# Masks in a row on GpSimd, a bank's last copy on ScalarE, fused gate terms, and attention parts emitted later, in a one-core streaming encoder step

## The chip, the cores and the metric

The kernel runs on one core of a Trainium2 chip. The metric is the device time of one execution in microseconds (us); the median of three runs is given with the lowest and highest. One execution was also recorded by the hardware profiler. Engines are named as in the profile: PE (TensorE matmul), PEld (its weight load), DVE (VectorE), ACT (ScalarE), POOL (GpSimd) and SP (SyncE, which issues the transfers).

## What is computed

One layer of an encoder runs on two request groups, 512 prompt rows and 64 sample rows (576 columns in the kernel), with shared weights in float32. The part that the change touches is the first third:

```python
xn = _rmsnorm(x, p['ln_mix'])
proj = xn @ p['w_in']
conv_in, z, a, b, qd, kd, vd = jnp.split(proj, SPLIT_AT, axis=-1)
c, conv_new = _causal_conv(conv_in, p['conv_w'], conv_buf)
c = jax.nn.silu(c.astype(jnp.float32))
...
g = -jnp.exp(p['a_log']) * jax.nn.softplus(a + p['dt_bias'])
beta = jax.nn.sigmoid(b)
oa, S_new = _gdn_chunked(qa, ka, va, g, beta, S0)
oa = _rmsnorm(oa, p['gdn_norm']) * jax.nn.silu(z)
```

`_gdn_chunked` is a gated delta rule over chunks of 64 rows: per chunk it forms products of keys, scales them with `exp` of differences of cumulated gates, and solves a lower triangular system. Behind it come a differential attention, the output projection, an attention over a memory of 256 rows (whose keys and values are projected here too), and a feed-forward block of width 4096.

## The kernel before

All activations stay on the chip, transposed: 128 features by 576 columns. Every weight matrix is read in tiles of 128x1024 and split into a high part (`wh`, a cast on ACT, L161) and a low part (`wl`, a subtraction on DVE, L162); a projection of 128 output columns is then three products, high by high, high by low and low by high. `project` (L170) does it in two halves, of 256 columns and of 320, each into a bank of the tag `pr`; there are three such banks. `evac` then takes a half out of its bank: the first half with a copy on ACT (L194) and an addition on DVE (L195), the second with two operations, on its first 256 and its last 64 columns.

The time line of the first third: the convolution's inputs are projected in blocks of 128 channels (`conv_input`, L314 to L323), each followed by the four convolution terms (ACT L455, DVE L457) and a silu (ACT L459, L460). Then the gates are computed from two small projections: softplus as an exponential (L525) and a series on DVE (L526 to L538), which ends in `gg` (L548), then cumulated sums on PE and exponentials for `beta`, `egl` and `kdc` (ACT L549, L569, L571, L590). Then four z blocks are projected (`project_z`, with the silu in L647 for a half's 256 columns and L649 for the last 64), with the memory's rows normed beside them (the squares in L223, transposes into `u` in L900). Beside the z blocks, `gdn_prep` prepares chunks two by two (c = 0 and 1 first): squares of keys and queries (ACT L682, L686), the exponential `gam` (ACT L701), the split of the system `At` (ACT L757), products on PE, and a solve that doubles block sizes from 1 to 64, for which a constant matrix `lev` of 128x128 holds at which level a pair of rows is joined (used in L734 and L764).

`lev` is built from masks of blocks of 2, 4, ... 128 rows. In the kernel before, POOL makes one mask (a fill and two affine selects, L605 to L608), DVE subtracts the one before (L610) and adds the difference to `lev` (L614), seven times.

The program's order is not the order in which the code emits it. A scheduler places the emitted instructions on the engines by dependence and its own costs; the code steers it with `tc.issue_after(i)` (what is emitted inside comes behind instruction i), `tc.high_priority()` and `tc.keep_in_program_order`. Each engine runs its own queue in order. On ACT, the functions come in table sets, and an ACT_TABLE_LOAD stands in the queue wherever the next function needs another set: silu and the exponential need different ones here, copies and squares need none.

Of the kernel before, what the change touches and what calls it, by code (L numbers as in the profile page):

```python
# [11 lines left out]
ALU = mybir.AluOpType  # L12
# [3 lines left out]
P = 128  # L16
# [3 lines left out]
DEC = 64  # L20
# [6 lines left out]
SOFF = 515  # L27
# [10 lines left out]
def hybrid_layer_kernel(  # L38
# [10 lines left out]
    V, A, G = nc.vector, nc.scalar, nc.gpsimd  # L49
# [29 lines left out]
    def nm(s):  # L79
        uid[0] += 1  # L80
        return f"{s}_{uid[0]}"

    def pair(slot, dt=F32):

        return up.tile([P, 2, 4, T], dt, tag=f"u{slot}", name=nm("u"))

    def view(u, i, a, b):
        return u[:, i].rearrange("p k t -> p (k t)")[:, : a * b].rearrange("p (a b) -> p a b", a=a)
# [3 lines left out]
    def small(tag, shape, bufs=None, dt=F32):  # L92
        tag = SHARED.get(tag, tag)
        bufs = 1 if tag in ("vn", "on", "S") or tag[:-1] in ("At", "Dt", "Y") else 2
        return sp.tile(shape, dt, tag=tag, name=nm(tag), bufs=bufs)
# [4 lines left out]
    def bank(tag="ba"):  # L100
        return ps.tile([P, 512], F32, tag=tag, name=nm(tag), bufs=BANKS[tag])

    def const(shape, name, dt=F32):
        return cp.tile(shape, dt, tag=name, name=name)
# [32 lines left out]
    ident = const([P, P], "ident")  # L137
# [17 lines left out]
    def split_weights(w, shape):  # L155
        raw = wp.tile(shape, F32, tag="raw", name=nm("raw"), bufs=3)
        nc.sync.dma_start(raw, w.rearrange("(k p) n -> p k n", p=P))
        wh = wp.tile(shape, F32R, tag="wh", name=nm("wh"))
        wl = wp.tile(shape, F32R, tag="wl", name=nm("wl"))
        with tc.high_priority():  # L160
            A.copy(wh, raw)  # L161
            V.tensor_tensor(wl, raw, wh.bitcast(F32), ALU.subtract)  # L162
        return wh, wl
# [29 lines left out]
    def add_to(dst, b, more):  # L193
        A.copy(dst, more)  # L194
        V.tensor_tensor(dst, b, dst, ALU.add)  # L195
# [116 lines left out]
    def conv_input(m, tag="cb"):  # L312
        cbs[m] = cb = small(tag, [P, 584])
        G.memset(cb[:, 0:3], 0.0)  # L314

        def evac(b, a0, n, more):
            if a0 == 0 and more is None:
                A.copy(cb[:, 3:259], b)
            elif a0 == 0:
                add_to(cb[:, 3:259], b, more)  # L320
            else:
                A.copy(cb[:, 3 + a0 : 259 + a0], b[:, :256])
                V.tensor_copy(cb[:, SOFF + 3 : SOFF + 3 + DEC], b[:, 256:])  # L323

        return evac

# [113 lines left out]
    for typ in (1, 0, 2):  # L440
# [3 lines left out]
        for h in range(H):  # L444
            m = typ * 4 + h
# [5 lines left out]
            cb = cbs[m]  # L451
# [6 lines left out]
            last_v = nc.cur_bb.bb.instructions[-1]  # L458
# [6 lines left out]
        if typ == 1:  # L465
            behind_keys = last_v, last_g
# [27 lines left out]
    for a0, n in HALVES:  # L494
        b = bank("pr")
# [7 lines left out]
    b = bank()  # L503
# [13 lines left out]
    def gt(tag):  # L517
        return const([P, 5, 4], tag)

    pre, gg, beta = gt("pre"), gt("gg"), gt("beta")  # L520
    t1, t2, t3 = gt("t1"), gt("t2"), gt("t3")
# [5 lines left out]
    V.reciprocal(t2, t2)  # L527
    V.tensor_tensor(t1, t1, t2, ALU.mult)
    V.tensor_tensor(t2, t1, t1, ALU.mult)
    V.tensor_scalar(t3, t2, 1.0 / 17, 1.0 / 15, ALU.mult, ALU.add)  # L530
    for d in (13, 11, 9, 7, 5, 3, 1):
        V.tensor_tensor(t3, t3, t2, ALU.mult)
        V.tensor_scalar(t3, t3, 1.0 / d, None, ALU.add)
    V.tensor_tensor(t3, t3, t1, ALU.mult)
    V.tensor_scalar(pre, pre, 0.0, None, ALU.max)
    V.scalar_tensor_tensor(t3, t3, 2.0, pre, ALU.mult, ALU.add)
    V.tensor_tensor(t3, t3, ea.unsqueeze(1).to_broadcast([P, 5, 4]), ALU.mult)
# [16 lines left out]
    for j in range(3):  # L554
        b = bank()
# [40 lines left out]
    mn = view(e5, 0, 2, D)  # L596
    mhl = pair(4, F32R)
    mh, ml = view(mhl, 0, KT, NMEM), view(mhl, 1, KT, NMEM)
    with tc.issue_after(behind_keys[0]), tc.issue_after(behind_keys[1]):
        lev = const([P, P], "lev")  # L600
        prev = ident
        for lb in range(7):
            s = 2 << lb
            e = small("X", [P, P])
            G.memset(e, 1.0)  # L605
            ev = e.rearrange("p (n s) -> p n s", s=s)
            G.affine_select(out=ev, in_=ev, pattern=[[-s, P // s], [0, s]], compare_op=ALU.is_ge, fill=0.0, base=0, channel_multiplier=1)  # L607
            G.affine_select(out=ev, in_=ev, pattern=[[s, P // s], [0, s]], compare_op=ALU.is_ge, fill=0.0, base=s - 1, channel_multiplier=-1)  # L608
            m = small("B0", [P, P])
            V.tensor_tensor(m, e, prev, ALU.subtract)  # L610
            if lb == 0:
                V.tensor_copy(lev, m)
            else:
                V.scalar_tensor_tensor(lev, m, float(1 << lb), lev, ALU.mult, ALU.add)  # L614
            prev = e

# [461 lines left out]
    for w, out in ((w_mem_k, o_mk), (w_mem_v, o_mv)):  # L1080
        dst = tokens
        for f in range(2):
            fs = slice(512 * f, 512 * f + 512)
            bs = [bank("pr") for _ in range(2)]
            for kc in range(4):
                wt = split_weights(w[0, 256 * kc : 256 * kc + 256, fs], [P, 2, 512])
                for k in (2 * kc, 2 * kc + 1):
                    for t in range(2):
                        ts_ = slice(t * P, (t + 1) * P)
                        for j, (wi, x) in enumerate(((0, mh), (0, ml), (1, mh))):  # L1090
                            mm(
                                bs[t], x[:, k, ts_], wt[wi][:, k % 2, :],
                                start=(k == 0 and j == 0), stop=(k == KT - 1 and j == 2),
                            )
            for t in range(2):
                (A.copy if t else V.tensor_copy)(dst[:, t, fs], bs[t])
                if out is o_mv:
                    A.copy(mv[:, t, fs], dst[:, t, fs])
                    V.tensor_tensor(mvl[2 * t + f], dst[:, t, fs], mv[:, t, fs].bitcast(F32), ALU.subtract)
            if out is o_mk:  # L1100
                for i in range(2):
                    b = bank()
                    for j in range(2):
                        m = 4 * f + 2 * i + j
                        for t in range(2):
                            tr(b[:, j * 256 + t * P : j * 256 + (t + 1) * P], dst[:, t, m * P : (m + 1) * P])
                    m = 4 * f + 2 * i
                    split_turned(mkT[:, m : m + 2, :], mkl[m // 2].rearrange("p (j n) -> p j n", j=2), b)
            nc.sync.dma_start(out[0, 0].rearrange("(b p) h d -> p b (h d)", p=P)[:, :, fs], dst[:, :, fs])
            if out is o_mk and f == 1:  # L1110
                finish()

                ob = pair(5, F32R)
                for h in range(H):
                    split_to((ob,), od[:, h, :], h, 0)
# [66 lines left out]
    for k2 in range(KT // 2):  # L1182
        b = bank()
# [6 lines left out]
    for h in range(H):  # L1190
# [15 lines left out]
        for t, (q0, _) in enumerate(QT):  # L1206
            t0, n = TT[t]
            kk, kl = (mkT, mkl) if t < 4 else (cmT, cml)
            b = bank(("gs", "g0", "g1")[t % 3])
            for i in range(2):  # L1210
                m, q = 2 * h + i, slice(q0, q0 + P)
# [23 lines left out]
        for i in range(2):  # L1235
            b, b2 = bank(("g0", "gs")[i]), bank(("g1", "ba")[i])
            fs = slice((2 * h + i) * P, (2 * h + i + 1) * P)
            for bi in range(2):
                m = 2 * h + i
# [334 lines left out]
    for m in range(KT):  # L1574
# [3 lines left out]
        if m in (3, 4):  # L1578
            t = m - 3
# [43 lines left out]
```

## Time and profile before

| | |
|---|---|
| median of 3 runs | 987.92 us (987.21 to 988.73) |
| the profiled execution | 987.2 us |
| its span | 985.5 us, granted clock 0.997 |
| PE busy | 968.5 us (98%) |
| DVE busy | 699.7 us (71%) |
| ACT busy | 530.1 us (54%) |
| POOL busy | 58.8 us (6%) |
| instructions | 16923 |

A row of the timeline in the profile has the start in us from the span's start, the time in us, the engine, the line of the kernel, the operation, the tile written and the tiles read, and in brackets how long the engine was idle just before and what ended that. A row of the groups has the count, the busy time and the mean of one in ns, then the idle time before them and what ended it.

### The profile page before, as it was taken

The page shows a single profiled execution, that of the slowest core. Times are in us where ns is not written, and L with a number is a line of the kernel's source. Part 1 is how long each engine was busy: PE and PEld are TensorE (multiplying, and loading weights), DVE is VectorE, ACT ScalarE, POOL GpSimd, SP SyncE. Part 2 cuts the span into 40 slices and gives each one's busy share as a digit, 9 for nine tenths or more (in the row PEclk, how much of TensorE's full clock was granted, in tenths as well). Part 3 has the DMA queues.
Part 4 walks back from the last instruction along what each step waited for, and adds up shares of the span by engine and source line. Part 5 has one row for each costly group of instructions (what it writes and reads, how often), then busy time and mean ns, then how long its engine had stood idle before and what let it go on. Part 6 is the DMA issues. An engine that isn't in the chain of part 4 may idle for free.

```text
span 985.5 us, 16923 instructions
## 1 busy us (share of the span) xinstructions
PE 968.5 (98%) x6403; PEld 891.2 (90%) x6403; DVE 699.7 (71%) x1570; ACT 530.1 (54%) x1194; POOL 58.8 (6%) x127
## 2 busy tenths in 40 slices
PE   9999999999999999999999999999999999999996
PEld 7989899898888878999999999999999999999996
DVE  6666787877676676666557977657867779978674
ACT  7545575344656665444445657665544445555444
POOL 3341011101000000000000000000000000000000
PEclk9999999999999999999999999999999999999998
DMA  7432340103222647333111414222222223223202
GB/s 212 129 119 65 90 138 23 43 23 103 81 68 68 203 131 227 95 94 99 44 44 58 127 54 127 86 86 86 86 87 86 86 86 86 86 86 86 65 23 96
DMA packets 121714, 90.75 MB, mean 92 GB/s; under 512 B 5564, under 2 KB 112206, under 8 KB 121122
## 3 DMA queue, kind: packets, MB, share of 16 engines
q1 hardware_dynamic: 121266, 89.03, 30.9%
q8 instruction: 50, 0.82, 0.3%
q10 hardware_dynamic: 368, 0.66, 0.2%
q14 instruction: 30, 0.25, 0.1%
HBM read 79.93 MB, written 9.75 MB: 91 GB/s over the span
## 4 chain that ended last, share of the span: by engine, by line
PE 83%; DVE 4%; issue 3%; POOL 2%; DMA 2%; ACT 2%; POOLq 0%; ACTq 0%; SPq 0%; DVEq 0%
PE pr L107 51%; PE g L107 12%; PE ba L107 10%; PE gs L107 6%; PE ba L113 3%; PE g L113 1%; POOL tg L208 1%; DMA r<-in_w_ff_dram 1%; DVE p L457 1%; DVE wl L162 0%; DMA grow<-gdram 0%; DMA raw<-in_w_ff_dram 0%; POOL X L607 0%; POOL X L608 0%; DVE on L809 0%
## 5 line engine op out<-in xcount | busy, mean ns | idle before, releaser
L107 PE MATMUL pr<-u,wh 128*128 128x320 f32 (+2 forms) x1240 | 328.7, 343 | 1.3 <-DVE p L323 1.2
L107 PEld LDWEIGHTS pr<-u,wh 128*128 128x128 f32 x1240 | 212.3, 188 | 18.0 <-DVE p L323 1.8
L107 PE MATMUL pr<-u,wl 128*128 128x256 f32 (+1 forms) x816 | 226.7, 302 | 0.0
L107 PEld LDWEIGHTS pr<-u,wl 128*128 128x128 f32 x816 | 149.9, 189 | 2.7 <-DVE wl L388 0.2
L162 DVE TENSOR_TENSOR wl<-raw,wh 128x1024 fp32r<-128x1024 f32 x65 | 79.4, 1223 | 41.3 <-ACT wh L161 41.0
L161 ACT CAST wh<-raw 128x1024 fp32r<-128x1024 f32 x65 | 68.1, 1048 | 65.7 <-PE pr L107 50.5
L107 PE MATMUL pr<-u,w2h 128*128 128x320 f32 (+1 forms) x384 | 98.5, 340 | 0.0
L1369 ACT CAST w2h<-r 128x512 fp32r<-128x512 f32 x56 | 34.7, 620 | 87.9 <-PE pr L107 85.3
L107 PE MATMUL pr<-f,w2h 128*128 128x320 f32 (+1 forms) x288 | 74.3, 340 | 0.1
L107 PEld LDWEIGHTS pr<-u,w2h 128*128 128x128 f32 x384 | 65.0, 188 | 4.5 <-ACT u L1452 0.3
L107 PE MATMUL pr<-u,w2l 128*128 128x256 f32 (+1 forms) x256 | 65.1, 295 | 0.0
L1454 DVE TENSOR_TENSOR u<-u,pr 128x256 f32<-128x256 f32 x96 | 42.3, 448 | 16.9 <-PE pr L107 16.2
L107 PE MATMUL ba<-u,wl 128*128 128x288 f32 x360 | 53.0, 296 | 0.4 <-ACT keep L1405 0.4
L107 PEld LDWEIGHTS pr<-f,w2h 128*128 128x128 f32 x288 | 48.7, 188 | 4.0 <-issue 1.1
L107 PEld LDWEIGHTS ba<-u,wl 128*128 128x128 f32 x360 | 49.2, 188 | 1.2 <-ACT keep L1405 1.1
L107 PE MATMUL pr<-f,w2l 128*128 128x256 f32 (+1 forms) x192 | 48.8, 295 | 0.0
L107 PEld LDWEIGHTS pr<-u,w2l 128*128 128x128 f32 x256 | 46.9, 188 | 1.5
L208 POOL TENSOR_TENSOR tiny<-tiny,nhalf 128x1 f32<-128x1 f32 (+4 forms) x10 | 8.7, 870 | 631.6 <-DVE tiny L1522 529.8
L1370 DVE TENSOR_TENSOR w2l<-r,w2h 128x512 fp32r<-128x512 f32 x56 | 38.5, 688 | 10.7 <-ACT w2h L1369 10.4
L107 PE MATMUL pr<-wh,u 128*128 128x512 f32 x128 | 41.4, 401 | 0.0
L1414 ACT ACTIVATE c<-c 128x288 f32<-128x288 f32 x48 | 20.6, 443 | 29.5 <-DVE c L1413 29.5
L107 PEld LDWEIGHTS pr<-f,w2l 128*128 128x128 f32 x192 | 35.2, 188 | 1.2
(514 smaller groups left out, 2025.1 us busy)
## 6 DMA issues: line engine op xcount, KB each, us to landing
raw<-in_w_ff_dram SPq DMA_DIRECT2D x36, 512.0 KB
raw<-in_w_in_dram SPq DMA_DIRECT2D x28, 512.0 KB
r<-in_w_ff_dram SPq DMA_DIRECT2D x56, 256.0 KB
raw<-in_w_mem_k_dram SPq DMA_DIRECT2D x8, 512.0 KB
raw<-in_w_mem_v_dram SPq DMA_DIRECT2D x8, 512.0 KB
raw<-in_w_out_dram SPq DMA_DIRECT2D x8, 512.0 KB
raw<-in_w_mem_q_dram SPq DMA_DIRECT2D x8, 512.0 KB
raw<-in_w_mem_o_dram SPq DMA_DIRECT2D x8, 512.0 KB
```

The source lines that it names most:

```text
L107: i = nc.tensor.matmul(out, lhsT, rhs, start=start, stop=stop, skip_group_check=skip_group_check)
L113: i = nc.tensor.transpose(out, in_, ident[:n, :n])
L161: A.copy(wh, raw)
L162: V.tensor_tensor(wl, raw, wh.bitcast(F32), ALU.subtract)
L208: G.tensor_tensor(out, in_, bc(nhalf[: in_.shape[0], 0:1], list(in_.shape)), ALU.pow)
L457: V.scalar_tensor_tensor(yv[:, :n], cb[:, i : i + n], cwt[:, m, i : i + 1], yv[:, :n], ALU.mult, ALU.add)
L1369: A.copy(wh, src)
L1370: V.tensor_tensor(wl, src, wh.bitcast(F32), ALU.subtract)
L1414: A.activation(c, c, AF.Relu)
L1454: V.tensor_tensor(am, am, b, ALU.add)
```

## The change

Four edits:

1. The last 64 columns of a convolution block's second half are copied out of the bank by ACT, not DVE.
2. The series of the gates takes a `scalar_tensor_tensor` a term (add a constant, then multiply), where there were a multiplication and an addition.
3. POOL makes six masks one after the other, kept in six tiles of 128x128. DVE combines them later, behind the last convolution block (`last_v`): `lev` starts as 64 minus the identity, and 2^lb times each mask is taken off it.
4. The split of one input of the output projection (`ob`) is emitted with another half of the memory's projection: `o_mv`, first half, instead of `o_mk`, second half.

```diff
             else:
                 A.copy(cb[:, 3 + a0 : 259 + a0], b[:, :256])
-                V.tensor_copy(cb[:, SOFF + 3 : SOFF + 3 + DEC], b[:, 256:])
+                A.copy(cb[:, SOFF + 3 : SOFF + 3 + DEC], b[:, 256:])
...
-    V.tensor_scalar(t3, t2, 1.0 / 17, 1.0 / 15, ALU.mult, ALU.add)
-    for d in (13, 11, 9, 7, 5, 3, 1):
-        V.tensor_tensor(t3, t3, t2, ALU.mult)
-        V.tensor_scalar(t3, t3, 1.0 / d, None, ALU.add)
-    V.tensor_tensor(t3, t3, t1, ALU.mult)
+    V.tensor_scalar(t3, t2, 1.0 / 17, None, ALU.mult)
+    for d in (15, 13, 11, 9, 7, 5, 3):
+        V.scalar_tensor_tensor(t3, t3, 1.0 / d, t2, ALU.add, ALU.mult)
+    V.scalar_tensor_tensor(t3, t3, 1.0, t1, ALU.add, ALU.mult)
...
-    with tc.issue_after(behind_keys[0]), tc.issue_after(behind_keys[1]):
-        lev = const([P, P], "lev")
-        prev = ident
-        for lb in range(7):
+    near_ = [t for u in (small("X", [P, 4, P]), small("X", [P, 4, P])) for t in (u[:, 0, :], u[:, 1, :], u[:, 2, :])]
+    with tc.issue_after(behind_keys[1]):
+        for lb, e in enumerate(near_):
             s = 2 << lb
-            e = small("X", [P, P])
             G.memset(e, 1.0)
...
-            m = small("B0", [P, P])
-            V.tensor_tensor(m, e, prev, ALU.subtract)
-            if lb == 0:
-                V.tensor_copy(lev, m)
-            else:
-                V.scalar_tensor_tensor(lev, m, float(1 << lb), lev, ALU.mult, ALU.add)
-            prev = e
+    lev = const([P, P], "lev")
+    with tc.issue_after(last_v):
+        V.tensor_scalar(lev, ident, -1.0, 64.0, ALU.mult, ALU.add)
+        for lb, e in enumerate(near_):
+            V.scalar_tensor_tensor(lev, e, -float(1 << lb), lev, ALU.mult, ALU.add)
...
             if out is o_mk and f == 1:
                 finish()
-
+            if out is o_mv and f == 0:
                 ob = pair(5, F32R)
                 for h in range(H):
                     split_to((ob,), od[:, h, :], h, 0)
```

The edits also change where the scheduler puts the instructions around them. Line numbers of the changed kernel are smaller by 3 to 5 from the masks on: its L642 and L644 are L647 and L649 before, L548, L568, L570 and L589 are L549, L569, L571 and L590, L677 is L682, L696 is L701, L752 is L757 and L895 is L900.

First place: ACT's queue around the gates' exponentials, where the second z block ends. `u` is here the silu's result, `pr` the bank of a half of a z block (in the changed kernel pr_1686 is of the first z block, pr_1739 of the second), `t`, `egl` and `kdc` belong to the gates. Before:

```order
L549 ACT_TABLE_LOAD
L549 ACTIVATE t_1160<-ab 128x20
L569 ACTIVATE egl<-ba_1230 128x20
L571 ACTIVATE kdc<-kdc 128x20
L590 ACTIVATE kdc_1194<-kdc_1194 128x2
L161 CAST wh_1850<-raw_1848 128x1024
L682 ACTIVATE B_168_1317<-g_166_1310 128x512
L682 ACTIVATE B_209_1487<-g_207_1480 128x512
L647 ACT_TABLE_LOAD
L647 ACTIVATE u_76<-pr_1768 128x256
L686 ACTIVATE B_170_1325<-g_169_1320 128x512
L686 ACTIVATE B_211_1495<-g_210_1490 128x512
```

And in the changed kernel:

```order
L548 ACT_TABLE_LOAD
L548 ACTIVATE t_1160<-ab 128x20
L642 ACT_TABLE_LOAD
L642 ACTIVATE u_76<-pr_1686 128x256
L568 ACT_TABLE_LOAD
L568 ACTIVATE egl<-ba_1223 128x20
L589 ACTIVATE kdc_1187<-kdc_1187 128x2
L644 ACT_TABLE_LOAD
L644 ACTIVATE u_76<-pr_1686 128x64
L161 CAST wh_1821<-raw_1819 128x1024
L570 ACT_TABLE_LOAD
L570 ACTIVATE kdc<-kdc 128x20
```

The four gate exponentials stood in a row behind one load; now the silus of the first z block stand between them, and each change of function has its load.

Second place: ACT's queue from the exponentials `gam` of chunks 0 and 1 to the silu that frees the bank for the fourth z block. Before:

```order
L701 ACT_TABLE_LOAD
L701 ACTIVATE Y_173_1338<-Y_173_1338 128x512
L701 ACTIVATE Y_213_1503<-Y_213_1503 128x512
L720 ACTIVATE B_222_1538<-grow_1246 128x512
L223 ACTIVATE u_78,tiny_1649<-u_76 128x1024
L161 CAST wh_2581<-raw_2579 128x1024
L757 COPY B_187_1386<-At_175_1349 128x256
L757 COPY B_190_1401<-At_175_1349 128x256
L647 ACT_TABLE_LOAD
L647 ACTIVATE u_76<-u_76 128x256
L647 ACTIVATE u_76<-pr_1821 128x256
L649 ACTIVATE u_76<-pr_1821 128x64
```

And in the changed kernel (the other `gam` exponential stands a few rows further ahead, with a load of its own):

```order
L642 ACT_TABLE_LOAD
L642 ACTIVATE u_76<-u_76 128x256
L696 ACT_TABLE_LOAD
L696 ACTIVATE Y_161_1309<-Y_161_1309 128x512
L161 CAST wh_2552<-raw_2550 128x1024
L715 ACTIVATE B_210_1509<-grow_1239 128x512
L895 CAST u_1250<-ba_1626 128x4x128
L895 CAST u_1250<-ba_1633 128x4x128
L223 ACTIVATE u_78,tiny_1640<-u_76 128x1024
L752 COPY B_175_1357<-At_163_1320 128x256
L644 ACT_TABLE_LOAD
L644 ACTIVATE u_76<-pr_1739 128x64
```

The two `gam` exponentials now have a load each, the memory's rows (L895, L223) stand between them and the silu, and the silu of the last 64 columns of the second z block (L644) comes last, behind a load of its own. The first matmul of the fourth z block waits for it, since it takes over that bank.

Third place: DVE's queue where the convolution blocks run, with the masks of before (`wl` is a weight's low part, `p` a convolution input or sum):

```order
L610 TENSOR_TENSOR B_161_1298<-X_1294,X_1287 128x128
L162 TENSOR_TENSOR wl_714<-raw_711,wh_713 128x1024
L323 COPY p_78_589<-pr_610 128x64
L614 SCALAR_TENSOR_TENSOR lev<-B_161_1298,lev 128x128
L610 TENSOR_TENSOR B_163_1305<-X_1301,X_1294 128x128
```

And DVE's queue at the gates in the changed kernel, where the masks `X` are combined now:

```order
L507 COPY ab_1148<-ba_1142 128x80
L608 TENSOR_SCALAR lev<-ident 128x128
L509 TENSOR_TENSOR ab<-ab_1148 128x40
L610 SCALAR_TENSOR_TENSOR lev<-X_1251,lev 128x128
L522 TENSOR_TENSOR pre<-ab,dtb 128x20
L558 COPY p_140_1210<-ba_1205 6x512
L523 TENSOR_SCALAR t_1160<-pre 128x20
L610 SCALAR_TENSOR_TENSOR lev<-X_1251,lev 128x128
L524 TENSOR_TENSOR t_1160<-t_1160,pre 128x20
L610 SCALAR_TENSOR_TENSOR lev<-X_1251,lev 128x128
```

The mask work leaves DVE's queue at the convolution blocks, and stands between the first operations of the gates.

## The prediction

> **What bounds the kernel now.** I read the page's first part, then the waits of PE, then the stretches in time, then the rows of single engines where the edits lie. The busy row of the page comes first.
>
> ```profile
> PE 968.5 (98%) x6403; PEld 891.2 (90%) x6403; DVE 699.7 (71%) x1570; ACT 530.1 (54%) x1194; POOL 58.8 (6%) x127
> ```
>
> PE is busy for 968.5 us of a span of 985.5, and PE's matmuls are the same in number and shape in both kernels. So the change can only take away what PE waits for, or add to it. What PE waits for is in its waits (engine, line, what it waited for, us in total, times, longest).
>
> ```profile
> PE g L113 <- DVE tg L713: 1.3, 1, 1.3
> PE pr L107 <- DVE p L323: 1.2, 2, 1.0
> PE pr L107 <- DVE wl L162: 0.8, 1, 0.8
> PE gs L107 <- DVE on L809: 0.8, 1, 0.8
> PE g L113 <- DVE KQ L709: 0.5, 1, 0.5
> PE gs L113 <- DVE on L809: 0.5, 1, 0.5
> PE ba L107 <- DVE gg L548: 0.5, 1, 0.5
> PE g L113 <- DVE Dt L772: 0.4, 1, 0.4
> PE g L107 <- DVE At L705: 0.4, 1, 0.4
> ```
>
> These rows sum to 6.4 us. Two of them name lines that the change touches: L323 (1.2 us) and the gates gg (0.5). No wait here is for ACT. Whether ACT has room is read by stretch: span of the stretch, then busy time of PE, PEld, DVE and ACT.
>
> ```profile
> 60.00:80.00 20.00, 19.79 (x125) 18.37 (x124) 14.57 (x23) 11.48 (x21) 4.24 (x12) 1.00 0.40 103
> 100.00:120.00 20.00, 19.54 (x131) 17.34 (x130) 15.42 (x57) 10.42 (x20) 0.36 (x2) 1.00 0.38 95
> 120.00:140.00 20.00, 19.52 (x142) 18.19 (x141) 17.56 (x50) 16.59 (x32) 3.88 (x3) 1.00 0.51 159
> ```
>
> ACT's 54% is an average. From 120 to 140 us, where the z projections run beside the preparation of chunks 0 and 1, ACT is busy for 16.59 us of 20: 3.41 us are free there, 9.58 in the stretch before it.
>
> **Edit 1, the last copy of a bank on ACT, and edit 3, the masks.** The rows of DVE around PE's longest wait for L323, and PE's row behind it:
>
> ```profile
> 57.35 0.29 DVE L610 TENSOR_TENSOR B<-X,X 128x128 f32<-128x128 f32 x1 [0.70 <-POOL X L608]
> 57.56 1.22 DVE L162 TENSOR_TENSOR wl<-raw,wh 128x1024 fp32r<-128x1024 f32 x1
> 58.69 0.22 DVE L323 COPY p<-pr 128x64 f32<-128x64 f32 x1
> 58.97 0.50 PE L107 MATMUL pr<-u,wh 128*128 128x512 f32 x1 [1.04 <-DVE p L323]
> ```
>
> The copy that frees the bank stands on DVE behind a 1.22 us split, which stands behind an L610 that waited for POOL. In the changed kernel the copy follows L322 on ACT, DVE has no mask work there, and both waits for L323 go: **-1.2 us** (1.04 and the rest of the waits' row). What could be late next is ACT's own chain. Twelve copies of 0.22 us enter ACT; one fits in 20 us with 8.5 us free (the row 60:80). If the copy came behind one of ACT's casts (near 1.05 us, rows below), the wait of 1.04 would stay and the gain be 0.2: ends -1.2 and -0.2. I take -1.2, since the new ACT order has L323 directly behind L322, which releases the same bank already.
>
> The masks themselves: POOL's groups, 7 masks before, 6 now.
>
> ```profile
> L607 POOL TENSOR_SCALAR_AFFINE_SELECT X<-X 128x128 f32<-128x128 f32 x7 | 3.4, 489 | 0.4
> L608 POOL TENSOR_SCALAR_AFFINE_SELECT X<-X 128x128 f32<-128x128 f32 x7 | 2.9, 409 | 0.4
> 51.94 0.20 POOL L452 COPY p<-gcol 128x3 f32<-128x3 f32 x1
> 60.73 0.42 DVE L195 TENSOR_TENSOR p<-pr,p 128x256 f32<-128x256 f32 x1
> ```
>
> In a row, three more masks (about 0.9 us each by the two groups, and a fill of 0.2) come ahead of the small copy L452, which then lands near 55.3 instead of 52.14. The first use of that buffer is the L195 at 60.73 and a later ACT row: 5 us of cover, cost 0; without the cover it would be these 3.2 us. On DVE the combination moves to the gates: 7 operations (a TENSOR_SCALAR and 6 SCALAR_TENSOR_TENSOR) at the 0.29 of L610, 2.0 us.
>
> **Edit 2, the gates.** One of its two groups on DVE, and two rows of it:
>
> ```profile
> L532 DVE TENSOR_TENSOR t<-t,t 128x20 f32<-128x20 f32 x7 | 1.3, 180 | 0.2
> 111.39 0.18 DVE L530 TENSOR_SCALAR t<-t 128x20 f32<-128x20 f32 x1
> 111.60 0.18 DVE L532 TENSOR_TENSOR t<-t,t 128x20 f32<-128x20 f32 x1
> ```
>
> One follows the other every 0.21 us; 7 fewer are 1.5 us off a chain that ends in gg, for which PE waits 0.5. But the 2.0 us of combining now stand in DVE's order ahead of the series, and an L162 split still stands inside it. The bounds on PE's wait there are 0 and twice the 0.5; I take no change, as 1.5 and 2.0 nearly cancel.
>
> **Edit 4, the attention parts.** From PE's 2612th row before the end on, about 325 us into the span, every engine's order is the same row for row in both kernels; the split L162 for which PE waits 0.8 (the row above) is in that stretch and stands where it stood. Cost 0, gain 0.
>
> **What moves with them: ACT's order and its table loads.** This is the term that decides. In the order, ACT_TABLE_LOADs go from 11 to 17. All six more lie between the softplus exponential (L525) and the end of the second z block, where the silu of the z blocks and the exponentials of the gates and of chunks 0 and 1 now alternate instead of standing in groups. The rows of before there:
>
> ```profile
> 115.71 0.42 ACT L647 ACTIVATE u<-u 128x256 f32<-128x256 f32 x1 [0.95 <-DVE u L195]
> 116.15 1.28 ACT L549 ACT_TABLE_LOAD   x1
> 117.44 0.22 ACT L549 ACTIVATE t<-ab 128x20 f32<-128x20 f32 x1
> ...
> 120.00 1.04 ACT L161 CAST wh<-raw 128x1024 fp32r<-128x1024 f32 x1
> 120.95 1.08 ACT L682 ACTIVATE B<-g 128x512 f32<-128x512 f32 x2
> 122.04 1.28 ACT L647 ACT_TABLE_LOAD   x1
> 124.67 0.40 ACT L194 COPY u<-pr 128x256 f32<-128x256 f32 x1
> 125.10 1.28 ACT L701 ACT_TABLE_LOAD   x1
> 126.75 0.63 ACT L701 ACTIVATE Y<-Y 128x512 f32<-128x512 f32 x1 [0.37 <-DVE Y L700]
> 128.93 1.05 ACT L223 ACTIVATE u<-u 128x1024 f32<-128x1024 f32 x1
> ```
>
> One load takes 1.28 us of ACT, and the next ACTIVATE starts at once (116.15 + 1.28 = 117.43). Six more are 7.7 us, against 3.41 free in 120:140.
>
> What PE needs from ACT there: three banks "pr" hold the z results, so the first matmul of a half block needs the bank of three halves earlier, which ACT's silu frees. In the changed order the silu of the second block's last 64 columns (L644) has a load of its own and stands 24 rows behind the cast that the end of that block lets go. The fourth block's first half needs its bank. PE's rows for the second block's end and the fourth's start, and rows that price transposes and products:
>
> ```profile
> 119.98 0.28 PE L107 MATMUL pr<-u,wl 128*128 128x256 f32 x1
> 121.59 1.14 PE L113 MATMUL g<-ident,u 128*128 128x128 f32 x8
> 122.49 0.48 PE L107 MATMUL pr<-u,wh 128*128 128x512 f32 x1
> 130.20 0.28 PE L107 MATMUL pr<-u,wl 128*128 128x256 f32 x1
> ```
>
> Before, the second block ends just ahead of 119.98 and the fourth starts at 130.20, with PE full between. Now step by step:
> 1. The second block's end comes at about 118.5: 119.98 less 1.2, and less some 0.3 of small products that now stand behind it.
> 2. From there ACT does, in its own order: two casts at 0.95 (120.00 to 120.95), six loads at 1.28, four squares at 0.54 (1.08 for two), five wide exponentials and copies at 0.53 (0.63 less the overlap of neighbours), two squares over 1024 elements at 1.15 with their sums, and six small copies and silus of 0.15 to 0.44, 1.9 together. That is 1.9 + 7.7 + 2.2 + 2.6 + 2.3 + 1.9 = 18.6.
> 3. So the bank is free at 118.5 + 18.6 = 137.1 at the earliest. With 2 us of waits inside (a copy out of a transpose stands in the row, and the transpose stands on PE behind a product that waits for DVE, which stands behind a POOL power) it is 139.1. I take the middle, 138.1.
> 4. PE has by then done more than before: 16 transposes and products of 128x128 that came later, 0.11 each (eight from 121.59 to 122.49), 1.7 us. The same work stood done before at 130.20 + 1.7 = 131.9.
> 5. So PE is behind by 5.2 to 7.2 us, 6.2 in the middle; the 1.2 gained is inside this, as step 1 starts from it. The wait of 0.5 for KQ, which came after 130.20, has run out behind PE's new wait: less 0.5. **+5.7.**
>
> The Trainium skill, "ScalarE: Activation LUTs", section "Table sets: the hidden batching unit", speaks against this order: calls should be batched by table set. Its section "What ACT_TABLE_LOAD costs" puts a switch at 1283 ns for the load and about 1380 ns for a drain. The load agrees with the 1.28 of this trace, the drain doesn't show: the row before the load ends at 116.13 and the one after it starts at 117.44. By the row the six loads are the 7.7 of step 2, by the page 16.0.
>
> **After 140 us.** Left are the waits for tg, Dt, At and on: 1.3 + 0.4 + 0.4 + 0.8 + 0.5 = 3.4 us. The chunks' solves start later, but PE has more of the projections left to put beside them. Bounds -2 and +2, a little over half of that 3.4 gone or added; I take -0.5.
>
> **Sum.** 5.7 - 0.5 = +5.2 us. Against the profiled execution of 987.2 (span 985.5) that is 992.4; the median of the runs lies 0.7 above that execution, so the time is **993.1**. A measurement of this kernel can tell about 0.2%, 2 us, from no change.
>
> **The rivals.**
> - *The loads are covered* (faster). A load waits for no data and can run while ACT would idle, and ACT has 13 us free from 100 to 140. PE alone would reach the fourth block at 118.5 + 10.2 + 1.7 = 130.4 (10.2 from 119.98 to 130.20), so this decides if step 2's row takes 11.9 us and not 18.6, with all but one of its loads off the path. Then the waits for L323, gg and KQ go (1.2 + 0.5 + 0.5) and 1.2 of the later 3.4: -3.4, 984.5. For it: no PE wait of before is for ACT. Against it: the loads stand between operations that follow each other without a gap before (120.00 to 126.38). Chance 0.19.
> - *Only L323 matters* (same). The z stage comes out even, the rest is hidden: -1.2, 986.7. Chance 0.10.
> - *The stall goes on* (slower, more). With chunks 0 and 1 late by 6 us, their last solve steps have less independent work beside them, and the later 3.4 us of waits double: 6.7 + 3.4 = +10.1, 998.0. Chance 0.13.
> - *POOL in a row is late.* The 5 us of cover of L452 go, and its 3.2 us come on top of the forecast: 996.3. For this the three masks would have to take three times their rows. Chance 0.03.
> - *A switch costs more than its row.* The longest idle time behind a load here is 0.37 (at 126.75); six of them are 2.2 on top, 995.3. Chance 0.01. With the drain of the Trainium skill's "ScalarE: Activation LUTs" ("What ACT_TABLE_LOAD costs") it would be six times 1.38, an estimate from that page: 8.3 on top, 1001.4.
>
> **How the numbers follow.** The forecast has 0.54, with a range of its own of 990.6 to 996.6: 5.2 - 0.5 - 2 and 7.2 - 0.5 + 2 on 987.9. It is slower over all of that. Slower: 0.54 + 0.13 + 0.03 + 0.01 = 0.71. Same: 0.10. Faster: 0.19. The range 985.0 to 997.0 holds the forecast, the even case, the late POOL, and two fifths each of the covered case and of the stall that goes on: 0.8.
>
> **What would show it.** Right: PE rows between 125 and 140 that wait for ACT, 5 us or more in all, the largest at the fourth z block's first matmul; ACT over 19 of 20 us busy from 120 to 140, with six loads more; no wait for L323 near 58 and 66. Wrong: PE full from 120 to 140, or waits for ACT below 2 us in all; a PE wait for POOL or L452 between 55 and 70; the wait of 0.8 for L162 gone.

## The result and the profile after

The changed kernel takes 997.56 us (median of 4 runs, 995.47 to 998.84) against 987.78 of the kernel before: a ratio of 1.0099, 95% interval 1.0087 to 1.0111, or +9.8 us. It was run twice more beside the kernel before: 995.54 against 987.29 (1.0075, 1.0058 to 1.0091) and 995.55 against 987.12 (1.0100, 1.0084 to 1.0115). The forecast was slower by 5.2, with a range up to 997.0: the direction came, the size did not. The first median lies above the range and the two repeats inside it, but all three grew by at least 8.3 us. The profiled execution took 998.77 (span 996.9).

The busy row of the page and what PE waits for:

```profile
PE 973.5 (98%) x6403; PEld 894.6 (90%) x6403; DVE 696.1 (70%) x1544; ACT 541.6 (54%) x1212; POOL 57.5 (6%) x124
```

```profile
PE g L113 <- ACT B L677: 4.6, 1, 4.6
PE g L107 <- DVE At L700: 1.7, 2, 1.1
PE ba L113 <- DVE u L233: 1.2, 1, 1.2
PE g L113 <- DVE Dt L767: 1.2, 1, 1.2
PE g L113 <- DVE KQ L704: 0.9, 1, 0.9
PE pr L107 <- DVE wl L162: 0.8, 1, 0.8
PE gs L107 <- DVE on L804: 0.7, 1, 0.7
```

The waits for L323 and gg are gone, and a wait of 4.6 us for ACT is new. PE's busy time grew by 5.0 us as well, with the same products: part of them ran slower (0.73 us against 0.46 for two of 128x320, in PE's rows below). The stretches say where (span, PE, PEld, DVE, ACT and POOL busy, granted clock, DMA):

```profile
100.00:120.00 20.00, 20.00 (x132) 17.66 (x131) 14.30 (x53) 14.50 (x20) 0.00 (x0) 1.00 0.33 85
120.00:140.00 20.00, 13.11 (x78) 12.06 (x76) 12.08 (x36) 15.38 (x24) 3.84 (x3) 0.83 0.41 129
140.00:160.00 20.00, 19.08 (x144) 17.59 (x143) 17.92 (x41) 13.26 (x36) 1.70 (x3) 1.00 0.10 27
```

Up to 120 us PE is full. From 120 to 140 it is busy 13.11 us of 20, where it was 19.52, and the granted clock falls to 0.83. ACT is idle there for 4.6 us too, though more loads stand in its row: it waits in its turn. Its rows, from the cast at the second z block's end to the silu that frees the bank (L644):

```profile
118.18 1.05 ACT L161 CAST wh<-raw 128x1024 fp32r<-128x1024 f32 x1 [0.49 <-ACT u L644]
119.25 1.28 ACT L570 ACT_TABLE_LOAD   x1
120.55 0.22 ACT L570 ACTIVATE kdc<-kdc 128x20 f32<-128x20 f32 x1
121.05 1.28 ACT L642 ACT_TABLE_LOAD   x1
122.34 0.39 ACT L642 ACTIVATE u<-pr 128x256 f32<-128x256 f32 x1
124.84 1.20 ACT L677 ACTIVATE B<-g 128x512 f32<-128x512 f32 x2 [2.12 <-DVE kd L675]
126.06 1.28 ACT L696 ACT_TABLE_LOAD   x1
...
133.64 0.63 ACT L696 ACTIVATE Y<-Y 128x512 f32<-128x512 f32 x1 [0.62 <-DVE Y L695]
135.77 1.05 ACT L161 CAST wh<-raw 128x1024 fp32r<-128x1024 f32 x1 [1.50 <-PE pr L107]
137.63 1.08 ACT L895 CAST u<-ba 128x512 fp32r<-128x512 f32 x2 [0.28 <-PE ba L113]
...
140.07 1.28 ACT L644 ACT_TABLE_LOAD   x1
141.36 0.23 ACT L644 ACTIVATE u<-pr 128x64 f32<-128x64 f32 x1
```

On DVE, the product kd that the squares wait for stands behind a gam operation of chunk 1, and that waits for a transfer (grow, the cumulated gates written to HBM and read back to all partitions):

```profile
119.27 1.22 DVE L162 TENSOR_TENSOR wl<-raw,wh 128x1024 fp32r<-128x1024 f32 x1 [2.98 <-ACT wh L161]
123.60 0.61 DVE L695 SCALAR_TENSOR_TENSOR Y<-grow,Gc,most 128x128 f32<-128x128 f32 x2 [3.10 <-DMA grow<-gdram]
124.13 1.28 DVE L675 TENSOR_TENSOR kd<-g,kdc 128x512 f32<-128x512 f32 x2
```

And PE's rows, with the wait, the slow products behind it, and the first product of the fourth z block at the end:

```profile
120.53 0.40 PE L107 MATMUL pr<-u,wh 128*128 128x512 f32 x1
125.50 1.12 PE L113 MATMUL g<-ident,u 128*128 128x128 f32 x4 [4.57 <-ACT B L677]
128.20 0.73 PE L107 MATMUL pr<-u,wh 128*128 128x320 f32 x2
133.32 0.46 PE L107 MATMUL pr<-u,wh 128*128 128x320 f32 x2
136.94 1.09 PE L113 MATMUL ba<-ident,u 128*128 128x128 f32 x8 [1.25 <-DVE u L233]
139.11 1.16 PE L107 MATMUL g<-u,u 128*128 128x128 f32 x8 [1.08 <-DVE At L700]
141.19 0.66 PE L113 MATMUL g<-ident,u 128*128 128x128 f32 x4 [0.92 <-DVE KQ L704]
141.64 0.50 PE L107 MATMUL pr<-u,wh 128*128 128x512 f32 x1
```

The fourth z block starts at 141.64, where it started at 130.20: 11.4 us later, which is as much as the span grew. The silu of L644 ends at 141.59, 0.05 us ahead of it. But PE does not stand idle for that silu: the four transposes ahead of the block waited for KQ on DVE, and they end at the same time. So two rows arrive together: ACT's up to the silu, and DVE's through gam, `u` and At to KQ. PE's idle time lies ahead, at the squares (4.57), `u` (1.25), At (1.08) and KQ (0.92).

### The profile page after: what moved, and what is told of

It is laid out like the page before. It is cut to its first block, busy times and chain, and to the rows that moved or that the text cites. A ratio compares the mean times of both kernels' runs of the same rounds, so it can differ in the third digit from the quotient of the medians.

```text
span 996.9 us, 16921 instructions
## 1 busy us (share of the span) xinstructions
PE 973.5 (98%) x6403; PEld 894.6 (90%) x6403; DVE 696.1 (70%) x1544; ACT 541.6 (54%) x1212; POOL 57.5 (6%) x124
## 4 chain that ended last, share of the span: by engine, by line
PE 86%; DVE 5%; issue 2%; ACT 2%; DMA 2%; POOL 1%; POOLq 0%; ACTq 0%; SPq 0%; DVEq 0%
PE pr L107 55%; PE g L107 11%; PE ba L107 9%; PE gs L107 6%; PE ba L113 3%; PE g L113 2%; DMA raw<-in_w_ff_dram 1%; POOL tg L208 1%; DMA r<-in_w_ff_dram 1%; DMA grow<-gdram 0%; DVE wl L162 0%; DMA gdram<-p 0%; ACT wl L1263 0%; ACT c L1409 0%; ACT c L1410 0%
## 5 line engine op out<-in xcount | busy, mean ns | idle before, releaser
L162 DVE TENSOR_TENSOR wl<-raw,wh 128x1024 fp32r<-128x1024 f32 x65 | 79.4, 1223 | 53.0 <-ACT wh L161 52.1
```

## The experiments

Three theories were set against each other. **A**: ACT's row with the alternating loads holds PE (through the silu that frees the bank, or through what DVE gets late from ACT). **B**: the transfer that holds DVE, and so the squares, makes the difference. **C**: half the granted clock behind a long wait does. Each kernel ran beside the kernel before on the same chip; times are medians, the difference is against the kernel before of that group. The last column is the start of the fourth z block in the profiled execution.

| kernel | loads | time, us | difference | fourth z block |
|---|---|---|---|---|
| before | 11 | 987.1 to 987.8 | | 130.20 |
| changed | 17 | 997.56, 995.54, 995.55 | +9.8, +8.3, +8.4 | 141.64, 139.62, 138.76 |
| edit 2 undone (no_gates) | 11 | 987.04 | -0.3 | 130.41 |
| edit 1 undone (no_copy) | 11 | 988.03 | +0.7 | 129.62 |
| edit 3 undone (no_masks) | 17 | 999.52 | +12.2 | 141.46 |
| kd first | 17 | 996.49, 998.20 | +9.2, +11.1 | 137.76, 137.92 |
| 36 products in the wait (fill) | 17 | 996.49 | +9.2 | 141.75 |
| 12 products in the wait (fill12) | 17 | 996.43 | +9.2 | 139.21 |
| silu left out (no_silu) | 5 | 990.21 | +2.9 | 131.70 |
| before, two loads more (ld2) | 13 | 987.86 | +0.6 | 130.25 |
| before, four loads more (ld4) | 15 | 996.45 | +9.2 | 141.05 |
| chunk 1's gam later (gam_late) | 15 | 990.88 | +3.8 | 133.06 |
| beta's exponential later (v_beta2) | 11 | 989.38 | +2.1 | 133.62 |
| both of these (v_beta3) | 11 | 985.47, 985.57 | -1.8, -1.6 | 127.94 |

**Which edits make the order.** Each of the first three edits was taken back by itself.

```diff
 no_gates: the series as in the kernel before
-        V.scalar_tensor_tensor(t3, t3, 1.0 / d, t2, ALU.add, ALU.mult)
+        V.tensor_tensor(t3, t3, t2, ALU.mult)
+        V.tensor_scalar(t3, t3, 1.0 / d, None, ALU.add)
...
 no_copy:
-                A.copy(cb[:, SOFF + 3 : SOFF + 3 + DEC], b[:, 256:])
+                V.tensor_copy(cb[:, SOFF + 3 : SOFF + 3 + DEC], b[:, 256:])
 no_masks: the masks as in the kernel before
-    near_ = [t for u in (small("X", [P, 4, P]), small("X", [P, 4, P])) for t in (u[:, 0, :], u[:, 1, :], u[:, 2, :])]
...
+            V.tensor_tensor(m, e, prev, ALU.subtract)
...
```

no_gates. 

> The changed kernel with edit 2 (the gates' series) undone. Its order has 11 table loads, grouped as before, and kd ahead of gam on DVE. Theories A and B both: the stall at the z blocks goes, and the waits for L323 stay gone: 986.5 (987.8 - 1.2). If the series itself cost the time (not the order), it would be the same 986.5, so this tells only whether edits 1 and 3 alone gain: a time of 988 or more would say that the gain of 1.2 us is lost elsewhere.

no_copy. 

> The changed kernel with edit 1 (the copy L323 on ACT) undone. 11 table loads, kd ahead of gam. Theories A and B: no stall at the z blocks. L323 stands on DVE without mask work ahead of it, but still behind a split of 1.2 us, so of the waits of 1.2 us some 0 to 0.7 stay: 986.6 to 987.3.

no_masks. 

> The changed kernel with edit 3 (the masks) undone. 17 table loads, gam ahead of kd on DVE, as in the changed kernel. Theories A and B: the stall stays, 996 to 998.5, and the clock falls. So edits 1 and 2 together make the order. A time near 988 would say that the masks' combination on DVE at the gates is the cause.

Without edit 2, or without edit 1, the order has 11 loads again and the 10 us are gone (ratios 0.9998, 0.9989 to 1.0008, and 1.0007, 0.9997 to 1.0016). Without edit 3 they stay, and PE waits 1.6 us for a weight's low part up to 60.37 on top. So it needs both the copies on ACT and the shorter series for the scheduler to interleave silus and exponentials; the masks have no part in it. Two times came above what was expected, no_copy by 0.7 us and no_masks by 1.0.

The profile of no_masks also parts the two rows that arrive together in the changed kernel:

```profile
140.24 0.22 ACT L648 ACTIVATE u<-pr 128x64 f32<-128x64 f32 x1
140.69 1.12 PE L113 MATMUL g<-ident,u 128*128 128x128 f32 x4 [0.78 <-DVE KQ L708]
141.46 0.78 PE L107 MATMUL pr<-u,wh 128*128 128x512 f32 x1
```

The silu that frees the bank (L648 here) is done at 140.46, and the fourth z block still starts 1.0 us later, behind the transposes that waited for KQ. There DVE's row is the later one, not the silu. That edits 1 and 3 alone would gain 1.2 us was not borne out by the time: 987.04 can't be told from before. Its profile is 1.4 us ahead at the wait for L162 behind the memory's projection (363.05 against 364.41), and gives 1.1 back behind it, where the order is the same.

Edit 4 was not run alone: with edits 1 to 3 and without it, every engine's order is that of the changed kernel, row for row, when buffer and line numbers are left out.

**Theory B, kd ahead of the transfer.**

```diff
         V.tensor_tensor(kd, bk, kdcc.unsqueeze(2).to_broadcast(wide), ALU.mult)
+        made = nc.cur_bb.bb.instructions[-1]
...
+        with tc.issue_after(made):
             for i in range(nb):
                 V.scalar_tensor_tensor(gam[:, i, :], bg[:, i, :], G_[:, i : i + 1], most, ALU.subtract, ALU.min)
```

> The changed kernel with one more order: DVE's two products kd (L675) come ahead of chunk 1's gam operations (L695 there), which wait for the transfer of grow. ACT's order and its 17 table loads stay. Theory A, the table loads alone hold PE: 997.6, the PE wait of 4.6 us for the squares B (L677) stays. Theory B, the transfer holds DVE and so the squares: they start 2.1 us earlier (ACT's idle time ahead of them), PE's wait falls from 4.6 to about 2.5, and as it is then short the granted clock stays at 1.0 and the 2.9 us of slow products go too: 997.6 - 5.0 = 992.6. Theory B without the clock: 995.5.

Every local step came: ACT's order in that stretch is the same, the squares start at 122.16, PE's wait for them is 2.3 us, and the fourth z block starts at 137.76. The time didn't follow: 996.49, where 992.6 or 995.5 was expected. The changed kernel was therefore run again, and in the last group both side by side.

> The changed kernel once more, on the chip of the runs sent with it, to compare them with: 997.6, with the PE wait of 4.6 us for the squares B and half the clock behind it.

> The changed kernel as the reference of this group: 995 to 998, with executions up to 3 us apart, as the transfer of grow lands earlier or later.

> The kernel with kd ahead of chunk 1's gam, beside the changed kernel on one chip. If the landing of grow sets the time where it lies on the path, this is 1 to 2 us below the changed kernel's median and its executions lie closer together. If ACT's row alone sets it, both medians agree within 1 us.

The changed kernel's second profile shows how much the transfer moves. DVE and PE rows of it:

```profile
121.62 0.61 DVE L695 SCALAR_TENSOR_TENSOR Y<-grow,Gc,most 128x128 f32<-128x128 f32 x2 [1.64 <-DMA grow<-gdram]
139.62 0.49 PE L107 MATMUL pr<-u,wh 128*128 128x512 f32 x1
```

The same program, with grow 2.0 us earlier (121.62 against 123.60), starts the fourth z block 2.0 us earlier, and that execution took 996.67 where the other took 998.77. Of these 2.0 us, 0.5 were there before the transfer (its write to HBM starts at 114.21 against 114.73); the write then took 1.99 us against 3.43, and the read as long in both (4.92 and 4.95). So in this pair the transfer's share is about 1.4 us. But kd first, which takes the transfer off that path, is no faster: 998.20 beside 995.55 (1 to 2 us less, or the same, was expected), ratios to before of 1.0112 (1.0098 to 1.0126) and 1.0100. It starts the fourth z block 0.8 us earlier (137.92 against 138.76) and reaches the wait for L162 behind the memory's projection 1.7 us later (373.26 against 371.61), since its later order on DVE and PE is another. As the cause of the 10 us, theory B fell; by the change of order that it needed, it can't be said what the transfer costs the median.

**Theory C, the clock.** Products were put on PE into the wait, so that it doesn't stand still.

```diff
+            def busy():
+                last = nc.cur_bb.bb.instructions[-1]
+                b = bank("gs")
+                with tc.issue_after(last), tc.high_priority():
+                    for i in range(12):
+                        mm(b[:, :P], triu, ones)
+            project(weights(w2, 1536 + h * P), xs, evac, between=busy if h == 2 else None)
-            project(weights(w2, 1536 + h * P), xs, evac)
```

With 36 products: 

> The changed kernel with 36 products of 128x128 more on PE (into a bank not used yet) behind the third z block's first half, where PE waits 4.6 us for the squares. They take about 4.0 us, in the wait. ACT's queue is the same up to the squares. Theory C (the clock falls because PE stands still): the granted clock stays at 1.0 from 118 to 135, and the products of the z block behind the wait take 0.15 us each, not 0.27; 2.9 us less for these, 994.7 if nothing else moved, though the order behind the squares is another (fewer loads there, 16), which may take 1 to 3 us more off. Rival (the clock falls for another reason, such as the transfers of that stretch): the clock falls as before.

With 12: 

> The changed kernel with 12 products of 128x128 more on PE (0.11 us for each of 24 passes by the run with 36, 2.7 us) in the wait for the squares. Up to the fourth z block every engine's order else is that of the changed kernel. Theory C (PE standing still brings half the clock): the clock stays at 1.0 behind it, and the 1.7 to 2.9 us of slow products go; the fourth z block starts earlier by what of this ACT does not take up (1.5 us of ACT's idle time there waited for PE): 994 to 996. If the clock falls all the same, theory C is wrong or 2 us of standing still are enough.

The 36 took 8.2 us and not 4.0 (each is two passes of 0.11), so they outlasted the wait and held PE themselves; the clock stayed at 1.0, as the theory has it, and the time is that of the changed kernel. With 12, granted clock and PE around the wait:

```profile
121.00:126.00 5.00, 4.69 (x40) 4.32 (x39) 3.27 (x8) 4.39 (x7) 0.00 (x0) 1.00 1.01 368
126.00:130.00 4.00, 3.37 (x26) 2.85 (x24) 1.33 (x5) 3.97 (x7) 1.67 (x1) 1.00 0.17 42
130.00:134.00 4.00, 2.94 (x21) 2.68 (x22) 4.00 (x14) 2.42 (x4) 0.77 (x2) 1.00 0.00 0
134.00:138.00 4.00, 1.94 (x16) 1.51 (x13) 3.67 (x11) 4.00 (x8) 1.44 (x1) 1.00 0.24 66
138.00:141.00 3.00, 2.56 (x9) 2.31 (x10) 2.57 (x8) 2.12 (x6) 0.00 (x0) 0.55 0.60 175
```

PE runs at full clock from 121 to 138, where the changed kernel has 0.50 from 126 to 130. That PE's standing still brings the half clock in this wait is shown. But the fourth z block starts at 139.21, inside the 138.76 to 141.64 of the changed kernel, right behind L644's end (139.16) and the transposes that waited for KQ. So the full clock put neither row ahead of what the changed kernel itself shows. What the clock costs in all is not measured, since it halves again from 138 (0.55). As the cause of the 10 us theory C fell; the times, 996.49 and 996.43, lie above the 994.7 and the 994 to 996 that it expected.

**Theory A, the loads.** First more of them in the kernel before, by a silu of 128x1 put between exponentials.

```diff
+        with tc.issue_after(held[-1]) if c == 1 else ExitStack():
             A.activation(gam, gam, AF.Exp)
+        if c == 0:
+            A.activation(turnover[:, 0:1], gam[:, 0, 0:1], AF.Silu)
+            held.append(nc.cur_bb.bb.instructions[-1])
...
 ld4 only, behind the squares of keys:
+        if c == 0:
+            A.activation(turnover[:, 1:2], sq[:, 0, 0:1], AF.Silu)
+            A.activation(turnover[:, 2:3], turnover[:, 1:2], AF.Exp)
```

ld2. 

> The kernel before with two table loads more between the gam exponentials of chunks 0 and 1 (a silu of 128x1 put between them, its result not used): 13 loads. Theory A: 2 x 1.28 + 0.2 = 2.8 us more on ACT, against 3.4 us free from 120 to 140: 0 to 2 us more, 987.3 to 989.3.

ld4. 

> The same with a second pair, between the squares of keys and queries: 15 loads, 5.5 us more on ACT against 3.4 free. Theory A: PE waits for ACT there, 2 to 5 us more, 989.3 to 992.3. Were loads covered by ACT's idle time elsewhere, it would be as ld2.

Two loads more cost 0.6 us (1.0006, 0.9997 to 1.0016), four cost 9.2 (1.0096, 1.0078 to 1.0114), twice the upper end of what was expected. The stretch and the rows of ld4 show where it stands:

```profile
120.00:140.00 20.00, 15.73 (x98) 13.82 (x97) 15.38 (x44) 18.44 (x28) 4.32 (x3) 0.84 0.51 158
```

```profile
139.48 1.28 ACT L649 ACT_TABLE_LOAD   x1
140.78 0.23 ACT L649 ACTIVATE u<-pr 128x64 f32<-128x64 f32 x1
```

```profile
132.33 1.16 PE L107 MATMUL g<-u,u 128*128 128x128 f32 x8 [2.18 <-DVE At L715]
134.79 1.11 PE L113 MATMUL g<-ident,u 128*128 128x128 f32 x4 [1.30 <-DVE KQ L719]
136.69 1.11 PE L113 MATMUL g<-ident,X 128*128 128x128 f32 x4 [0.79 <-DVE vb L727]
```

Only in ld4 has the silu of the second z block's last 64 columns moved behind the exponentials, behind a load of its own, as in the changed kernel; it ends at 141.0 and the fourth z block starts at 141.05. As in the changed kernel, PE is not idle right there: it waited before that for At, KQ and vb on DVE, and ran at half the clock from 134 to 138. In ld2 the silu stands where it stood (at 124.6), and two loads fit into ACT's idle time. So the price is no fixed sum per load. The next kernel keeps a count of 15 and changes the place: chunk 1's gam operations come behind chunk 0's on DVE, which also moves that silu forward.

```diff
+        with tc.issue_after(scaled[0]) if c == 1 else ExitStack():
             for i in range(nb):
                 V.scalar_tensor_tensor(gam[:, i, :], bg[:, i, :], G_[:, i : i + 1], most, ALU.subtract, ALU.min)
+        scaled.append(nc.cur_bb.bb.instructions[-1])
```

> The changed kernel with chunk 1's gam operations behind chunk 0's on DVE, nothing else asked for. ACT's order has 15 loads, but the silu that frees the bank for the fourth z block (L644) stands 13 rows behind the cast and not 24, with 2 loads ahead of it and not 6. If what stands ahead of that silu on ACT sets the time, it falls to 987 to 990 although four more loads than before are in the order. If the number of loads itself sets it, 994 to 996.

```profile
118.33 1.05 ACT L161 CAST wh<-raw 128x1024 fp32r<-128x1024 f32 x1 [0.52 <-ACT u L644]
128.53 0.22 ACT L644 ACTIVATE u<-pr 128x64 f32<-128x64 f32 x1
```

With 15 loads, as many as ld4, it takes 990.88 (1.0038, 1.0025 to 1.0051): the silu is done 10.4 us after the cast, not 23.4. The fourth block starts at 133.06; PE waited before it for an addition on DVE (1.64) and for the squares of the queries on ACT (1.28). The time is 0.9 us above the 987 to 990 expected. So the count of loads does not set the time, and what stands behind them does. Whether that is the silu or DVE's row, these kernels don't separate: this edit moves both.

The silu left out altogether: 

> The changed kernel with the silu of the z blocks left out (a plain copy of the projection instead), so ACT has 5 table loads in the whole program, none at the z blocks. Theory A: no stall at the z blocks, 985 to 986.5. If the copies moved to ACT and the order of DVE cost the time, 990 or more.

Here the z blocks hold plain copies, so their silu is missing from the output. The stall is gone (131.70), but 990.21 is 4 us over the expectation. Of the 2.6 us that its span is longer, 0.8 stand at the wait for L162 behind the memory's projection, and 1.8 come after it, where the order is the same as before. There PE waits 0.8 us for `keep` (0.4 before) and 1.1 for the `u` of L1451 (none listed before), 1.5 more; what brings these waits is not explained.

**The order put right.** Beta's exponential was the one that the shorter series had moved ahead of the first z block's silus.

```diff
-    A.activation(t1, ab[:, :, 4:8], AF.Exp, scale=-1.0)
-    V.tensor_scalar(t1, t1, 1.0, None, ALU.add)
-    V.reciprocal(beta, t1)
-    halves_of(beta2, beta)
...
     A.activation(kdc2, kdc2, AF.Exp)
+    shifted = nc.cur_bb.bb.instructions[-1]
+    with tc.issue_after(shifted):
+        A.activation(t1, ab[:, :, 4:8], AF.Exp, scale=-1.0)
+        V.tensor_scalar(t1, t1, 1.0, None, ALU.add)
+        V.reciprocal(beta, t1)
+        halves_of(beta2, beta)
```

> The changed kernel, all four edits, with one order more: the exponential for beta (L548) and what hangs on it come behind the last exponential of the gates on ACT (kdc of the sample). ACT's order then has 11 table loads in the old groups. kd stands between no waits for the transfer on DVE. Theory A (the alternating loads, the scheduler's order) : the stall at the z blocks goes, 986.5, as in the kernel with the gates' edit undone (987.0). Theory that the edits themselves cost (more ACT work, fewer and wider steps on DVE): 992 or more. Half the clock shows in neither.

One order takes six loads and 6.2 us away (989.38 beside 995.54), though 986.5 was expected. Left is a PE wait of 2.4 us for chunk 0's gam, which stands on DVE behind chunk 1's (waiting for grow) and behind an operation that waits for POOL:

```profile
121.92 1.14 DVE L697 SCALAR_TENSOR_TENSOR Y<-grow,Gc,most 128x128 f32<-128x128 f32 x4 [1.46 <-DMA grow<-gdram]
125.64 0.16 DVE L709 TENSOR_TENSOR tg<-tg,tg 128x4 f32<-128x4 f32 x1 [1.57 <-POOL tg L208]
125.87 1.12 DVE L697 SCALAR_TENSOR_TENSOR Y<-g,Gc,most 128x128 f32<-128x128 f32 x4
```

With the edit of gam_late on top, both stand behind chunk 0's gam:

> All four edits, the beta exponential behind the gates' last one, and chunk 1's gam operations (which wait for the transfer of grow) behind chunk 0's on DVE. 11 table loads. Theory B, in the form that DVE's queue held by the transfer costs PE 2.4 us and then half the clock for 3 us: both go, 989.4 - 4 = 985.5 to 986. If 989 stays, the operations that wait for POOL's power ahead of gam cost it, not the transfer.

> The version with the beta exponential and chunk 1's gam later, once more with more rounds: 985.5, below the kernel before by 1 to 2 us.

985.47 and 985.57, ratios 0.9989 (0.9979 to 0.9998) and 0.9985 (0.9976 to 0.9994): this version beats both kernels, the one before by 0.1 to 0.2%. Both edits together take the stall away, and PE is full again in this stretch:

```profile
120.00:140.00 20.00, 19.27 (x142) 18.30 (x142) 17.18 (x50) 14.77 (x30) 4.30 (x3) 1.00 0.48 145
```

Taken together: without the alternating order most or all of the 10 us go (no_gates, no_copy, v_beta2), and loads put ahead of the same rows bring them (ld4). So the order on ACT is the cause. Which of the two rows behind it holds PE, the bank's silu or DVE's row, stays open in the changed kernel.

## Why the prediction was right and wrong

- **Edits 1 and 3**: as worked out. No wait near 58 and 66 is left. The masks in a row put the buffer's small copy at 56.12, not 55.3, and nothing waited for it.
- **Edit 2**: taken as no change; the wait of 0.5 for gg went. The second z block ended at 118.17, against 118.5 in step 1.
- **Edit 4**: no effect, as said; the wait of 0.8 for L162 stayed.
- **Step 2, ACT's row**: 18.6 us of work were summed. The changed kernel has three profiles, with spans of 996.9, 994.7 and 993.0. The first has 141.59 - 118.18 = 23.4 us, of which 2.12 + 0.62 + 1.50 + 0.28 = 4.5 idle: 18.9 of work. Right.
- **Step 3, its waits**: this is the term that was mis-sized most. Between 0 and 2 us were given for them, 1 taken, by one chain. Measured are 4.5 in the first profile, 0.66 + 0.57 + 1.50 + 0.28 = 3.0 in the second and 0.72 + 0.89 + 0.42 = 2.0 in the third. Two were not seen: the gam operation of chunk 1 ahead of kd on DVE, which waits for grow (2.12, 0.66 and 0.72 on ACT), and the cast that waits for PE's half block (1.50 in the first two). So the bank was free at 141.6, 139.6 and 138.7, not 138.1. In the kernel with kd first, where the first of them is gone, it was 137.7.
- **Step 5, the path**: the start of the fourth block was put down to the bank alone. The silu ends 0.05 to 0.06 us ahead of that start in all three profiles, but DVE's row through KQ ends there too, and in no_masks it is the later one. That ACT's row alone gave the right place is in part luck.
- **Step 4 and the credits behind it**: 1.7 us of work done ahead, 0.5 for KQ and 0.5 of the later waits were credited, 2.7 in all. From the fourth z block to the wait for L162 the lag falls from 11.4 to 10.1 us in the first profile and from 9.4 to 8.1 in the second: 1.3. KQ takes 0.9, now ahead of the block; of the 3.4 us of later waits 3.2 are left.
- **The rest** is behind L162, where the order is one and the same: 1.3, 1.1 and 0.3 us more than in the profile of before. In the first two most of it is PE's waits for `keep` on ACT and for the `u` of L1451 (1.0 and 0.9 us for `keep` where it was 0.4, and 0.5 for `u`). (The wait for `keep`, 0.4 us before, is for ACT; the prediction says that there was none.) Over all profiled executions of all kernels that stretch took 620.2 to 622.9 us, so this is no cost of the change that could be told.
- **The sum, closed**: forecast, waits of step 3, missing credits, rest. The span grew by 5.2 + 3.5 + 1.4 + 1.3 = 11.4 us in the first profile, by 5.2 + 1.5 + 1.4 + 1.1 = 9.2 in the second, and by 5.2 + 0.6 + 1.3 + 0.3 = 7.4 (7.5 measured) in the third, where the bank was free within the bounds of step 3.
- **The clock** was not in the prediction. It halved for 6 us in the first profile; by fill12 that did not set the start of the fourth block.
- **The signs**: six loads more and no wait for L323 came. PE's waits for ACT were 4.6 us, not 5, and at the squares, not at the fourth z block's first matmul; ACT was busy for 15.38 us of 20, not over 19, since it waited too.
- **The rivals**: "the stall goes on" gave 998.0, next to the first median, but by a mechanism that isn't there, since the later waits did not double (3.2). "The loads are covered" is what ld2 shows for two loads; it fails in ld4, where rows that PE needs come behind them. "A switch costs more than its row": no, behind the loads whose data is there the next activation starts within 0.02 us (119.25 + 1.28 and 120.55).

The rule of the Trainium skill, "ScalarE: Activation LUTs", section "Table sets: the hidden batching unit", to batch by table set, points the right way (v_beta2 against the changed kernel, 6.2 us). But the price here does not go by the count of loads: 13 loads cost 0.6 us, which can't be told from none, 15 loads 3.8 or 9.2.

## What to carry to other kernels

Sum the row of the engine that frees a buffer from the event that starts it to the operation that frees it, and then list every wait inside that row on the other queues too: each operation ahead of the one waited for on its engine, and whether that one waits for a transfer. Look also whether the engine that waits would have come there sooner at all. Work taken off one engine can cost more through the order that a scheduler makes of it than through itself; here one constraint on one small exponential, and another on a row that waits for a transfer, turned +9 us into -1.7.

## What was not expected of the hardware

- PE's granted clock fell to about 0.5 behind waits of 4.57, 3.1 and 3.2 us (the changed kernel), 2.3 (kd first) and 2.4 (v_beta2), and in fill12 behind scattered waits of 1.2, 1.6 and 0.9 us with work between them. It stayed low for 3 to 6 us, while PE was full. In gam_late waits of 1.6 and 1.3 us did not do it, and one of 2.5 us in no_masks did not either. The Trainium skill, "TensorE: Matmul & The Clock Gate", section "Part 1: The HAM clock gate (the "warmup" mystery)", has the half rate after an idle window of about 3.4 us, and the full rate after a busy one of that length. The slow stretches of 3 to 6 us fit the second only roughly, and against the first, waits of 2.3 and 2.4 us were enough in two kernels.
- The way of grow through HBM landed 2.0 us apart in two executions of one program, 1.4 of it in the write of its 10 KB, and the time moved with it. The changed kernel's executions lie between 993.8 and 998.9, the kernel before's between 986.1 and 989.1.
